# State space steps of an encoder layer: the impulse response moves into the beat of the transposes and outputs

## The chip, the core and the metric

The kernel runs on one core of a Trainium2 chip. The metric is the device time of one execution in microseconds, from start to end of the program on that core; lower is better. The core has a matrix engine (TensorE, PE in the profile, with its weight loads shown apart as PEld), a vector engine (VectorE, DVE), an activation engine (ScalarE, ACT), a general engine (GpSimd, POOL) and an engine that here only issues transfers (SyncE, SP). Each runs its own queue of instructions in order; semaphores tie the queues together.

## The reference

One layer of an encoder is applied to 256 prompt tokens and 512 sample tokens, width 1024. One projection of the normalised input feeds three mixers: a state space model in both directions, differential attention, and attention into 256 memory tokens. Their outputs are weighted by gates and joined, and a feed-forward part follows. The change touches the state space model and runs beside the projection for the gates:

```python
def layer(x, mem, li, ...):
    h = rmsnorm(x, norm_mix_g[li])
    proj = h @ w_in[li]
    u, q, k, v, qm, gl = jnp.split(proj, SPLITS, axis=-1)
    ug = uf.reshape(Bsz, L, S5_GROUPS, S5_GROUP)      # 64 groups of 16 channels
    y_f = s5_direction(ug, ...)                       # forward in time
    y_b = jnp.flip(s5_direction(jnp.flip(ug, axis=1), ...), axis=1)
    y = (y_f + y_b).reshape(Bsz, L, S5_WIDTH) + s5_d[li].astype(F32) * uf
    ...

def s5_direction(u, lam_re, lam_im, log_dt, b_re, b_im, c_re, c_im):
    ...
    bu = jnp.einsum('bcgh,gph->bcgp', u_chunk.astype(jnp.complex64), b_bar)
    a_cum, s = lax.associative_scan(_lin_op, (a, bu), axis=1)   # 64 complex states per group
    y = jnp.einsum('bcgp,ghp->bcgh', s, c).real
```

## The kernel before

Tokens are cut into blocks of eight (96 blocks). Within a block the model is a small matrix, the impulse response; from block to block the states are carried by a scan. The 64 groups are done four at a time, in 16 steps numbered 0 to 15. In class `S5` each step has these parts:

- `fetch` loads the parameters (`par`, three buffers) by SP.
- `build` and `build_e` make the outer products `G` and `E` on VectorE, about six operations of 0.6 to 1.2 us each.
- `response` multiplies `G` with the input matrices on TensorE, 16 matmuls on tiles of 64 rows by 32 columns into two PSUM tiles `psK` (one for each direction). ScalarE copies both into `K`, VectorE adds the diagonal with two short operations, SP stores `K` to memory and reads it back eight times, shifted, as the block matrix `TT`.
- `weights` transposes `E` on TensorE into two PSUM tiles `psE`; ScalarE copies them into `ET`.
- `tables` makes the factors of the scan on ScalarE: `w` and `wr` (four instructions each), `R` (four), `cs` and `sn` (three). `R` has one buffer, so that the next step's `R` is written only when the scan of the step at hand has read it.
- `states` multiplies the inputs by `ET` (8 matmuls into `psI`, one pair of PSUM banks). VectorE rotates the result (`X`, `T`), scans it (`W`, two operations) and rotates it back.
- `outputs` multiplies by `TT` and `G` (12 matmuls into `psY`); ScalarE copies `psY` to `Ysb`, and SP stores it.

`steps` is a generator that strings these together for neighbouring steps and yields three times a round: it calls such a stretch a beat. The first beat of round `s` holds `response(s+1)` and `build_e(s+1)`, the second `states(s)` and `build(s+2)`, the third `outputs(s-1)`, `weights(s+1)` and `tables(s+1)`.

Beside the steps runs the projection for the gates: 72 groups of 24 matmuls (`gl`, 8 slices of the width times three products of high and low halves, 256 tokens wide). A group fills one PSUM bank of a pool of two, ScalarE copies it to `glt` with the bias added, SP stores it. After each group `pace.tick` lets the generator advance by 0.69 beats on average. The weights for `gl` come through `wr`, which ScalarE turns into a high and a low half (`wh`, `wl`, 128x1024 each), two pairs for six groups.

The written order is not the order in which the engines work. A scheduler takes the program as written and orders each engine's queue by when it holds an instruction to be ready; the queues below show what came of it. `keep_in_program_order` ties an instruction behind the one written just before it on its engine. The PSUM tiles `psK`, `psE` and `psY` come from one pool of four banks (`psum(1, b=4, w=1, d=2)`: four banks `b`, one pair `w` for `psI`, two `d` for `u` and `gl`).

Of the kernel before, what the change touches and what calls it, by code (L numbers as in the profile page):

```python
# [20 lines left out]
NK = 99  # L21
# [3 lines left out]
class S5:  # L25
# [313 lines left out]
    def build_e(self, qd):  # L339

        st = self.st[qd]
        st["E"] = self._outer("E", qd, 1, st["B"], st["F"], False)

    def response(self, qd):

        nc, pq, env = self.nc, self.pq, self.env
        st = self.st[qd]
        G = st["G"]

        psK = [env.psb(f"psK{qd}{d}") for d in range(2)]  # L350
        for w in range(2):
            for d in range(2):
                p = slice(64 * d, 64 * d + 64)
                for g in range(4):
                    c = 32 * g + 16 * w
                    nc.tensor.matmul(psK[d][32 * g : 32 * g + 32, 0:128], st["b"][p, c : c + 32],
                                     G[p, w, g].rearrange("p i h -> p (i h)"), start=(w == 0), stop=(w == 1))
        K = pq.tile([128, 240], F32, name=f"K{qd}", tag="K", bufs=1)
        nc.scalar.activation(K[:, 112:240], psK[0][:, 0:128], AF.Copy)
        nc.scalar.activation(K[:, 0:112], psK[1][:, 0:112], AF.Copy)  # L360
        k0 = K[:, 112:128]
        nc.vector.tensor_tensor(out=k0, in0=k0, in1=psK[1][:, 112:128], op=ALU.add)
        nc.vector.tensor_tensor(out=k0, in0=k0, in1=st["diag"], op=ALU.add)
        nc.sync.dma_start(self.k_scr[qd], K)
        kv = self.k_scr[qd].rearrange("(g r) c -> r g c", r=32)[0:16]

        TT = pq.tile([128, 4, 128], F32, name=f"TT{qd}", tag="TT", bufs=3)
        for j in range(8):
            nc.sync.dma_start(TT[16 * j : 16 * j + 16], kv[:, :, 16 * j : 16 * j + 128])
        st["TT"] = TT  # L370

    def weights(self, qd):

        nc, pq, env = self.nc, self.pq, self.env
        st = self.st[qd]
        E = st["E"]
        ET = pq.tile([128, 2, 4, 128], F32, name=f"ET{qd}", tag="ET", bufs=2)
        for c in range(2):
            ps = env.psb(f"psE{qd}{c}")
            for g in range(4):  # L380
                nc.tensor.transpose(ps[:, 128 * g : 128 * g + 128], E[:, c, g], env.ident)
            nc.scalar.activation(ET[:, c].rearrange("p g l -> p (g l)"), ps, AF.Copy)
        st["ET"] = ET

# [30 lines left out]
    def states(self, qd):  # L415
        nc, pq, env = self.nc, self.pq, self.env
        st = self.st[qd]
        mul, add, sub = ALU.mult, ALU.add, ALU.subtract
        vt = lambda o, a, b, op: nc.vector.tensor_tensor(out=o, in0=a, in1=b, op=op)
        mt, q = divmod(qd, 2)  # L420
        if q == 0:
            U = pq.tile([128, 8, NK], F32, name=f"U{mt}", tag="U", bufs=2)
            nc.sync.dma_start(U.rearrange("p g k -> p (g k)"), self.u_scr[mt])
            self.U = U
        U, ET = self.U, st["ET"]
        st["U"] = U
        sn, cs, R = st["tab"]
        ps = env.ps2(f"psI{qd}")
        for c in range(2):
            for g in range(4):  # L430
                nc.tensor.matmul(ps[:, c, NK * g : NK * g + NK], ET[:, c, g], U[:, 4 * q + g],
                                 start=True, stop=True)
        n = 4 * NK
        B3 = [128, 2, n]
        new = lambda tag, bufs: pq.tile(B3, F32, name=f"{tag}{qd}", tag=tag, bufs=bufs)

        X, T = new("X", 3), new("T", 1)
        vt(X, ps[:, :, 0:n], cs.unsqueeze(1).to_broadcast(B3), mul)
        vt(T, ps[:, ::-1, 0:n], sn, mul)
        vt(X, X, T, add)  # L440

        W = new("W", 1)
        Xf, Wf = (x.rearrange("p c k -> p (c k)") for x in (X, W))
        m, f, b = 2 * n, slice(0, 64), slice(64, 128)
        nc.vector.tensor_tensor_scan(out=Wf[f, 1:m], data0=R[f, 0 : m - 1], data1=Xf[f, 0 : m - 1],
                                     initial=0.0, op0=mul, op1=add)
        nc.vector.tensor_tensor_scan(out=Wf[b, m - 2 :: -1], data0=R[b, m - 1 : 0 : -1],
                                     data1=Xf[b, m - 1 : 0 : -1], initial=0.0, op0=mul, op1=add)

        S, T = new("X", 3), new("T", 1)  # L450
        i = slice(1, n - 1)
        vt(S[:, :, i], W[:, :, i], cs[:, i].unsqueeze(1).to_broadcast([128, 2, n - 2]), mul)
        vt(T[:, :, i], W[:, ::-1, i], sn[:, ::-1, i], mul)
        vt(S[:, :, i], S[:, :, i], T[:, :, i], add)
        S = [S[:, c].rearrange("p (g k) -> p g k", g=4)[:, :, 1:98] for c in range(2)]
        st["S"] = S

    def outputs(self, qd, y_scr):
        nc, pq, env = self.nc, self.pq, self.env
        st = self.st.pop(qd)  # L460
        mt, q = divmod(qd, 2)
        i = slice(1, 98)
        U, TT, S = st["U"], st["TT"], st["S"]
        G = st["G"]
        psY = env.psb(f"psY{qd}")
        for g in range(4):
            o = psY[:, 97 * g : 97 * g + 97]
            nc.tensor.matmul(o, TT[:, g], U[:, 4 * q + g, i], start=True, stop=False)
            nc.tensor.matmul(o, G[:, 0, g], S[0][:, g], start=False, stop=False)
            nc.tensor.matmul(o, G[:, 1, g], S[1][:, g], start=False, stop=True)  # L470
        Ysb = pq.tile([128, 4 * 97], F32, name=f"Ysb{qd}", tag="Ysb", bufs=2)
        nc.scalar.activation(Ysb, psY[:, 0 : 4 * 97], AF.Copy)

        nc.sync.dma_start(y_scr[mt][:, 388 * q : 388 * q + 388], Ysb)
# [5 lines left out]
    def steps(self, y_scr):  # L480

        self.st = {}
        n = 16

        def do(f, qd, *a):
            if 0 <= qd < n:
                f(qd, *a)

        for s in range(-3, n + 1):
            do(self.fetch, s + 3)  # L490
            if s < -2:
                continue
            do(self.response, s + 1)
            do(self.build_e, s + 1)
            yield
            do(self.states, s)
            do(self.build, s + 2)
            yield
            do(self.outputs, s - 1, y_scr)
            do(self.weights, s + 1)  # L500
            do(self.tables, s + 1)
            yield

# [1718 lines left out]
```

## Time and profile before

| | us |
|---|---|
| median of 3 runs | 1717.4 (1714.82 to 1717.45) |
| profiled execution | 1715.9 |
| its span, first to last instruction | 1714.1 |
| the stretch in which the state space steps run | about 255 to 590 |
| TensorE busy in 285 to 400, 400 to 500, 500 to 590 | 113.85, 99.45, 89.85 |
| VectorE busy in the same | 104.92, 92.60, 59.55 |
| ScalarE busy in the same | 84.44, 63.47, 45.64 |

A row of the timeline has the start, the length (both in us), the engine, the line, the operation, what is written from what, and how many were merged; brackets hold the idle time before it and who ended that. A row of the waits has who waited for whom, the sum, how many times, and the longest. In the trace a matmul of 32-bit type (`psI`, `psY`, `psK`) appears as two entries, so 8 of them read x16. The granted clock of TensorE is 1.00 throughout. A matmul's length in the trace is modelled; the distance between starts says how fast they follow each other.

### The profile page before, as it was taken

To read this page: it belongs to the slowest core of one execution; us is meant where nothing else is said; L and a number is where in the kernel's file an instruction comes from. 1 tells how busy PE (TensorE), PEld (TensorE's weight loads), DVE (VectorE), ACT (ScalarE), POOL (GpSimd) and SP (SyncE) were. 2 spreads that over 40 slices of the span, in tenths; PEclk is the share of its full clock that TensorE was granted. 3 is DMA by queue.
4 is the path that set the end of the run, shared out by engine and by line. 5 is a ranking of instruction groups with operands and counts; after the bars stand their busy time and mean duration, and the time that the engine had idled before them with its cause. 6 is when DMAs were issued, how large, how long until landed. Compare 5 with 4: busy or idle time off the path is not lost.

```text
span 1714.1 us, 31468 instructions
## 1 busy us (share of the span) xinstructions
PE 1700.2 (99%) x12082; PEld 1624.3 (95%) x12082; DVE 1313.2 (77%) x2383; ACT 931.8 (54%) x1957; POOL 337.1 (20%) x403
## 2 busy tenths in 40 slices
PE   9999999999999999999999999999999999999999
PEld 9999988999999999999989999998889898989897
DVE  6876556999997459889876687792698868687876
ACT  6554536766665357778766564552444545454541
POOL 0040510000000111001210111430114334343420
PEclk9999999999999999999999999999999999999999
DMA  8433456676656446565964445672314448484733
GB/s 298 166 97 102 136 170 151 153 187 176 170 152 165 129 108 144 132 154 135 209 134 131 162 148 171 153 214 72 87 49 115 137 113 192 114 192 115 173 119 108
DMA packets 206758, 250.02 MB, mean 146 GB/s; under 512 B 34272, under 2 KB 162800, under 8 KB 206608
## 3 DMA queue, kind: packets, MB, share of 16 engines
q1 hardware_dynamic: 162896, 155.70, 30.0%
q0 software_dynamic: 32480, 67.01, 20.5%
q10 hardware_dynamic: 11232, 25.31, 4.3%
q8 instruction: 95, 1.56, 0.4%
q14 instruction: 55, 0.45, 0.1%
HBM read 173.51 MB, written 52.17 MB: 132 GB/s over the span
## 4 chain that ended last, share of the span: by engine, by line
PE 81%; issue 10%; DMA 4%; DVE 3%; ACT 1%; POOL 0%; SPq 0%; POOLq 0%; ACTq 0%; DVEq 0%
PE br L846 4%; PE br L847 4%; PE br L848 4%; PE up L846 3%; PE up L847 3%; PE up L848 3%; PE gate L847 3%; PE gate L848 3%; PE gate L846 3%; PE dn L846 3%; PE dn L848 3%; PE dn L847 3%; PE qk L847 3%; PE qk L846 3%; PE qk L848 3%
## 5 line engine op out<-in xcount | busy, mean ns | idle before, releaser
L846 PE MATMUL gl<-Hhi,wh 128*128 128x256 f32 x576 | 164.7, 286 | 0.5 <-ACT glt L1264 0.3
L847 PE MATMUL gl<-Hlo,wh 128*128 128x256 f32 x576 | 160.4, 278 | 0.0
L848 PE MATMUL gl<-Hhi,wl 128*128 128x256 f32 x576 | 160.2, 278 | 0.0
L679 ACT ACTIVATE wh<-wr 128x1024 fp32r<-128x1024 f32 x116 | 122.3, 1056 | 51.7 <-PE u L847 10.8
L683 POOL DMA_DIRECT2D wl<-wr x46 | 40.2, 874 | 463.5 <-ACT wl L682 440.3
L685 DVE TENSOR_TENSOR wl<-wr,wh 128x1024 fp32r<-128x1024 f32 x70 | 85.8, 1227 | 38.7 <-ACT wh L679 37.1
L846 PEld LDWEIGHTS gl<-Hhi,wh 128*128 128x128 f32 x576 | 108.4, 188 | 3.4 <-issue 1.8
L848 PEld LDWEIGHTS gl<-Hhi,wl 128*128 128x128 f32 x576 | 108.8, 189 | 0.0
L847 PEld LDWEIGHTS gl<-Hlo,wh 128*128 128x128 f32 x576 | 108.4, 188 | 0.2 <-issue 0.2
L846 PE MATMUL qk<-wh,Hhi 128*128 128x256 f32 x384 | 107.6, 280 | 0.0
L847 PE MATMUL qk<-wl,Hhi 128*128 128x256 f32 x384 | 107.5, 280 | 0.0
L848 PE MATMUL qk<-wh,Hlo 128*128 128x256 f32 x384 | 107.2, 279 | 0.0
L602 ACT ACTIVATE wh_S<-ws 128x512 fp32r<-128x512 f32 x91 | 53.9, 625 | 67.0 <-PE up L847 27.8
L607 DVE TENSOR_TENSOR wl_S<-ws,wh_S 128x512 fp32r<-128x512 f32 x91 | 67.0, 757 | 28.9 <-ACT wh_S L602 28.8
L846 PEld LDWEIGHTS qk<-wh,Hhi 128*128 128x128 f32 x384 | 72.3, 188 | 0.8
L848 PEld LDWEIGHTS qk<-wh,Hlo 128*128 128x128 f32 x384 | 72.3, 188 | 0.5
L847 PEld LDWEIGHTS qk<-wl,Hhi 128*128 128x128 f32 x384 | 72.2, 188 | 0.5
L1436 ACT ACTIVATE p<-sc,nm 128x512 f32<-128x512 f32 (+1 forms) x96 | 59.0, 617 | 13.2 <-DVE nm L1434 12.8
L1434 DVE TENSOR_REDUCE nm<-sc 128x1 f32<-128x512 f32 (+1 forms) x96 | 56.7, 599 | 11.5 <-PE sc L1428 10.5
L628 POOL TENSOR_TENSOR ws<-wr,ws 128x512 f32<-128x512 f32 x26 | 38.8, 1492 | 126.1 <-DVE wl_S L607 106.8
L602 ACT ACTIVATE wh_A<-wr 128x512 fp32r<-128x512 f32 x65 | 38.1, 623 | 39.0 <-PE up L847 17.3
L1264 ACT ACTIVATE glt<-gl,bg 128x256 f32<-128x256 f32 x72 | 33.6, 466 | 46.4 <-PE gl L848 34.8
(704 smaller groups left out, 6324.9 us busy)
## 6 DMA issues: line engine op xcount, KB each, us to landing
wl<-wr POOLq DMA_DIRECT2D x46, 512.0 KB, 5.6
wr<-in_w_gate_up_dram SPq DMA_DIRECT2D x44, 512.0 KB, 4.1
wr<-in_w_in_dram SPq DMA_DIRECT2D x40, 512.0 KB, 4.8
wr<-in_w_branch_dram SPq DMA_DIRECT2D x24, 512.0 KB, 3.9
wr<-in_w_down_dram SPq DMA_DIRECT2D x22, 512.0 KB, 4.4
gl_scr<-glt SPq DMA_DIRECT2D x72, 128.0 KB, 3.6
wr<-in_w_in_dram SPq DMA_DIRECT2D x32, 256.0 KB, 4.4
wr<-in_w_mem_kv_dram SPq DMA_DIRECT2D x14, 512.0 KB, 5.1
```

The lines of the kernel that those rows point to most:

```text
L602: self.nc.scalar.activation(f(hi), src, AF.Copy)
L607: self.nc.vector.tensor_tensor(out=f(lo), in0=src, in1=f(hi).bitcast(F32), op=ALU.subtract)
L628: gt(out=s4, in0=A12, in1=s2, op=sub)
L679: self.nc.scalar.activation(hi, r, AF.Copy)
L683: self.nc.gpsimd.dma_start(lo, r.bitcast(F32R), accum_op=ALU.add)
L685: self.sub.tensor_tensor(out=lo, in0=r, in1=hi.bitcast(F32), op=ALU.subtract)
L846: pe.matmul(ps, wh, xh, start=start, stop=False)
L847: pe.matmul(ps, wh, xl, start=False, stop=False)
L848: pe.matmul(ps, wl, xh, start=False, stop=stop)
L1264: act.activation(gt[:, 0:n], ps[:, 0:n], AF.Identity, bias=bg[:, M : M + 1])
L1434: v.tensor_reduce(out=nm[:, m : m + 1], in_=ps, axis=AX.X, op=ALU.max, negate=True)
L1436: act.activation(pm[:, 0:n], ps, AF.Exp, bias=nm[:, m : m + 1], accum_out=s1s[:, tt : tt + 1] if m == 0 else s2)
```

## The change

`response(s+1)` leaves the first beat and is written last among TensorE's parts in the third, which now reads `weights(s+1)`, `outputs(s-1)`, `response(s+1)`, `tables(s+1)`. The matmuls of the state space steps are tied to the one written before them on TensorE, by a new helper `pe`; only in the first rounds, while the first third beat is set up, is the first of them left free. Later `gl` matmuls are not tied and can be ordered between.

```diff
+    def pe(self, i):
+
+        if self.joined:
+            self.tc.keep_in_program_order(i)
+        self.joined = True
+
     def response(self, qd):
...
-                    nc.tensor.matmul(psK[d][32 * g : 32 * g + 32, 0:128], st["b"][p, c : c + 32],
-                                     G[p, w, g].rearrange("p i h -> p (i h)"), start=(w == 0), stop=(w == 1))
+                    self.pe(nc.tensor.matmul(psK[d][32 * g : 32 * g + 32, 0:128], st["b"][p, c : c + 32],
+                                             G[p, w, g].rearrange("p i h -> p (i h)"), start=(w == 0), stop=(w == 1)))
...
-                nc.tensor.transpose(ps[:, 128 * g : 128 * g + 128], E[:, c, g], env.ident)
+                self.pe(nc.tensor.transpose(ps[:, 128 * g : 128 * g + 128], E[:, c, g], env.ident))
...
-                nc.tensor.matmul(ps[:, c, NK * g : NK * g + NK], ET[:, c, g], U[:, 4 * q + g],
-                                 start=True, stop=True)
+                self.pe(nc.tensor.matmul(ps[:, c, NK * g : NK * g + NK], ET[:, c, g], U[:, 4 * q + g],
+                                         start=True, stop=True))
...
-            nc.tensor.matmul(o, TT[:, g], U[:, 4 * q + g, i], start=True, stop=False)
-            nc.tensor.matmul(o, G[:, 0, g], S[0][:, g], start=False, stop=False)
-            nc.tensor.matmul(o, G[:, 1, g], S[1][:, g], start=False, stop=True)
+            self.pe(nc.tensor.matmul(o, TT[:, g], U[:, 4 * q + g, i], start=True, stop=False))
+            self.pe(nc.tensor.matmul(o, G[:, 0, g], S[0][:, g], start=False, stop=False))
+            self.pe(nc.tensor.matmul(o, G[:, 1, g], S[1][:, g], start=False, stop=True))
...
             if s < -2:
                 continue
-            do(self.response, s + 1)
             do(self.build_e, s + 1)
             yield
             do(self.states, s)
             do(self.build, s + 2)
             yield
+            self.joined = s > -1
+            do(self.weights, s + 1)
             do(self.outputs, s - 1, y_scr)
-            do(self.weights, s + 1)
+            do(self.response, s + 1)
             do(self.tables, s + 1)
             yield
```

What the queues make of it shows best in step 9. In the rows below, a name's first number is the step (`psK90` and `psK91` are the two response tiles of step 9); the last number only counts tiles. TensorE before, around the response of step 9:

```order
L847 MATMUL gl_489_5949<-Hlo_106,wh21_1_5427 128x256
L848 MATMUL gl_489_5949<-Hhi_105,wl21_1_5428 128x256
L356 MATMUL psK90_490_5979<-G9_5862,par9_5490 32x128 x7
L356 MATMUL psK91_491_5980<-G9_5862,par9_5490 32x128 x4
L356 MATMUL psK90_490_5979<-G9_5862,par9_5490 32x128
L356 MATMUL psK91_491_5980<-G9_5862,par9_5490 32x128 x4
L846 MATMUL gl_493_6020<-Hhi_105,wh21_0_5420 128x256
L847 MATMUL gl_493_6020<-Hlo_106,wh21_0_5420 128x256
```

TensorE after, the end of the outputs of step 7 and the response of step 9:

```order
L474 MATMUL psY7_498_6128<-U3_5528,TT7_5668 128x97
L475 MATMUL psY7_498_6128<-X7_5824,G7_5301 128x97
L476 MATMUL psY7_498_6128<-X7_5824,G7_5301 128x97
L362 MATMUL psK90_499_6144<-G9_5829,par9_5490 32x128 x4
L362 MATMUL psK91_500_6145<-G9_5829,par9_5490 32x128 x4
L362 MATMUL psK90_499_6144<-G9_5829,par9_5490 32x128 x4
L362 MATMUL psK91_500_6145<-G9_5829,par9_5490 32x128 x4
L853 MATMUL gl_502_6200<-Hhi_105,wh22_0_5737 128x256
```

The response stood alone between `gl` groups; now it follows the transposes of step 9 and the outputs of step 7, and three `gl` groups without a break follow it. On ScalarE before, from the table `R` of step 9 to the copies of the second `gl` group behind the transposes:

```order
L404 ACTIVATE R9_6180<-s5kmask_3589,s5rho_111 128x2x99 x4
L472 ACTIVATE Ysb7_6161<-psY7_498_6148 128x388
L382 ACTIVATE ET9_6164<-psE90_499_6165 128x512
L411 ACTIVATE cs10_6442<-wr10_6441,half_pi_87 128x396
L382 ACTIVATE ET9_6164<-psE91_500_6171 128x512
L409 ACTIVATE sn10_6444<-w10_6440 128x396 x2
L403 ACTIVATE wr11_6692<-s5kpos_3588,s5magic_3590,s5v8_110 128x99 x4
L1264 ACTIVATE glt_501_6199<-gl_502_6200,bg_112 128x256
L402 ACTIVATE w11_6691<-s5kpos_3588,s5v8_110 128x99 x4
L1264 ACTIVATE glt_503_6227<-gl_504_6228,bg_112 128x256
```

The same place on ScalarE after:

```order
L388 ACTIVATE ET9_6115<-psE90_496_6116 128x512
L388 ACTIVATE ET9_6115<-psE91_497_6122 128x512
L410 ACTIVATE R9_6180<-s5kmask_3589,s5rho_111 128x2x99 x4
L478 ACTIVATE Ysb7_6141<-psY7_498_6128 128x388
L365 ACTIVATE K9_6162<-psK90_499_6144 128x128
L417 ACTIVATE cs10_6442<-wr10_6441,half_pi_87 128x396
L366 ACTIVATE K9_6162<-psK91_500_6145 128x112
L409 ACTIVATE wr11_6692<-s5kpos_3588,s5magic_3590,s5v8_110 128x99 x2
L415 ACTIVATE sn10_6444<-w10_6440 128x396 x2
L409 ACTIVATE wr11_6692<-s5kpos_3588,s5magic_3590,s5v8_110 128x99 x2
L408 ACTIVATE w11_6691<-s5kpos_3588,s5v8_110 128x99 x4
L1271 ACTIVATE glt_501_6199<-gl_502_6200,bg_112 128x256
```

`ET` moved ahead of `R`, the two copies `K` and the four `w` moved between `R` and the first `glt`. In the steps where the beat comes two `gl` groups after `psI` (`R4`, `R5`, `R7`, `R10`, `R13`) `ET` stays behind `R`. In those of `R3`, `R7` and `R14` two `wh` and a `wl` stand between `R` and the first `glt` after the response as well, in that of `R9` none. TensorE after, in step 4, one of seven whose response is cut by `gl` matmuls (before, `psK40` and `psK41` stood together):

```order
L476 MATMUL psY2_431_4863<-X2_4533,G2_4040 128x97
L362 MATMUL psK40_432_4879<-G4_4538,par4_4199 32x128 x4
L853 MATMUL gl_435_4935<-Hhi_105,wh18_0_4294 128x256
L854 MATMUL gl_435_4935<-Hlo_106,wh18_0_4294 128x256
L855 MATMUL gl_435_4935<-Hhi_105,wl18_0_4295 128x256
L362 MATMUL psK41_433_4880<-G4_4538,par4_4199 32x128 x4
L362 MATMUL psK40_432_4879<-G4_4538,par4_4199 32x128 x4
L362 MATMUL psK41_433_4880<-G4_4538,par4_4199 32x128 x4
```

Three `gl` matmuls moved between the two tiles of the response; in steps 2, 4, 5, 6, 7, 10 and 13 it is 18, 3, 3, 15, 3, 29 and 6 of them. TensorE's order is the old one again from the end of this stretch on. On SP the stores of `K`, `glt` and `Ysb` and the loads of `TT`, `par` and `wr` change places among each other in it; GpSimd's queue is the same.

## The prediction

> **What bounds the kernel now.** I read the page first: the span, the share of each engine and the shares of the chain that ended last.
>
> ```profile
> span 1714.1 us, 31468 instructions
> PE 1700.2 (99%) x12082; PEld 1624.3 (95%) x12082; DVE 1313.2 (77%) x2383; ACT 931.8 (54%) x1957; POOL 337.1 (20%) x403
> PE 81%; issue 10%; DMA 4%; DVE 3%; ACT 1%; POOL 0%; SPq 0%; POOLq 0%; ACTq 0%; DVEq 0%
> ```
>
> TensorE has work for the whole span, so a change counts only where it lengthens or shortens TensorE's own queue: its matmuls, their spacing, and its stops. The order of the program changes only from 255 to 590 us, where the state space steps run inside the gate projection (`gl`). So I asked next who waits for whom in that stretch.
>
> ```profile
> ACT R L404 <- DVE W L447: 37.7, 13, 4.2
> DVE X L419 <- PE psI L431: 19.1, 9, 8.3
> PEld psK L356 <- ACT Ysb L472: 2.1, 3, 1.2
> PE psK L356 <- ACT Ysb L472: 1.4, 2, 1.0
> PEld gl L846 <- ACT glt L1264: 1.2, 3, 0.4
> PE gl L846 <- ACT glt L1264: 0.3, 2, 0.2
> 400.00:500.00 100.00, 99.45 (x986) 97.13 (x986) 92.60 (x111) 63.47 (x148) 6.90 (x8) 1.00 0.65 163
> ```
>
> The first two rows are the loop to keep in mind. VectorE waits for `psI`, ScalarE's table `R` waits for VectorE's scan `W`, 13 times, and everything behind `R` in ScalarE's queue waits with it. The next four are what this costs TensorE today: `psK` lacks a free PSUM bank until `Ysb` is copied out, and `gl` lacks one until `glt` is. The load rows alone give 2.1 + 1.2 = 3.3 us, all four 5.0, with some time counted twice; I take 4.2. The last row (TensorE, weight load, VectorE, ScalarE, GpSimd) has VectorE at 93%: nearly full, but not the bound.
>
> Then one step on TensorE, row by row, and the same step on ScalarE.
>
> ```profile
> 434.89 1.92 PE L431 MATMUL psI<-U,ET 128*128 128x99 f32 x16
> ...
> 439.44 0.35 PE L468 MATMUL psY<-U,TT 128*128 128x97 f32 x2
> ...
> 442.09 1.04 PE L381 MATMUL psE<-ident,E 128*128 128x128 f32 x8
> 442.88 0.36 PE L846 MATMUL gl<-Hhi,wh 128*128 128x256 f32 x1
> 443.08 0.28 PE L847 MATMUL gl<-Hlo,wh 128*128 128x256 f32 x1
> ...
> 448.50 0.28 PE L848 MATMUL gl<-Hhi,wl 128*128 128x256 f32 x1
> 448.71 0.67 PE L356 MATMUL psK<-G,par 64*32 64x128 f32 x32
> 449.50 0.39 PE L846 MATMUL gl<-Hhi,wh 128*128 128x256 f32 x1
> 449.73 0.28 PE L847 MATMUL gl<-Hlo,wh 128*128 128x256 f32 x1
> ...
> 452.23 0.28 PE L848 MATMUL gl<-Hhi,wl 128*128 128x256 f32 x1
> ```
>
> ```profile
> 443.43 1.52 ACT L404 ACTIVATE R<-s5kmask,s5rho 128x198 f32<-128x198 f32 x4 [3.26 <-DVE W L447]
> 444.85 0.47 ACT L472 ACTIVATE Ysb<-psY 128x388 f32<-128x388 f32 x1
> 445.22 0.58 ACT L382 ACTIVATE ET<-psE 128x512 f32<-128x512 f32 x1
> 445.70 0.61 ACT L411 ACTIVATE cs<-wr,half_pi 128x396 f32<-128x396 f32 x1
> 446.22 0.58 ACT L382 ACTIVATE ET<-psE 128x512 f32<-128x512 f32 x1
> 446.70 0.95 ACT L409 ACTIVATE sn<-w 128x396 f32<-128x396 f32 x2
> 447.55 1.54 ACT L403 ACTIVATE wr<-s5kpos,s5magic,s5v 128x99 f32<-128x99 f32 x4
> 448.99 0.46 ACT L1264 ACTIVATE glt<-gl,bg 128x256 f32<-128x256 f32 x1
> 449.35 1.18 ACT L402 ACTIVATE w<-s5kpos,s5v 128x99 f32<-128x99 f32 x4
> 450.42 0.47 ACT L1264 ACTIVATE glt<-gl,bg 128x256 f32<-128x256 f32 x1
> 450.78 0.27 ACT L359 ACTIVATE K<-psK 128x128 f32<-128x128 f32 x1
> 450.94 0.26 ACT L360 ACTIVATE K<-psK 128x112 f32<-128x112 f32 x1
> ```
>
> `R` starts 443.43 - 434.89 = 8.54 us after `psI` began: that is when `W` is done. The `glt` behind it ends at 448.99 + 0.46 = 449.45, and at 449.50 the third `gl` group since the transposes starts. It has two PSUM banks to share with its neighbours, and the gap before it is 0.2 us more than after other `psK` groups. So this walk along ScalarE's queue predicts a TensorE stop to within 0.1 us, and I use it on the new order.
>
> **The change, part by part.** No instruction is added or removed: 16 response, transpose, output and state steps stay, with their copies and DMAs. Four things move.
>
> *One: the old waits of `psK` (gain 4.2 us).* Now the largest looks like this:
>
> ```profile
> 354.52 0.63 PE L356 MATMUL psK<-G,par 64*32 64x128 f32 x14
> 356.12 0.64 PE L356 MATMUL psK<-G,par 64*32 64x128 f32 x18 [0.96 <-ACT Ysb L472]
> ```
>
> In the new order the fifth tile of the four-bank pool waits for the transposes' copy `ET` instead of `Ysb`. Where one `gl` group stands between `psI` and the beat, `ET` now stands ahead of `R` on ScalarE and is done about psI + 6, long before `psK` at psI + 8. Where two groups stand there, `ET` comes behind `R`, at psI + 8.5 + 1.4 + 0.4 + 0.5 = 10.8, and `psK`'s second tile comes at about 11, mostly with a few `gl` matmuls put in ahead. So this wait goes, and the `gl` stops are counted anew below.
>
> *Two: what is late next is `glt` (cost 9.3 us).* After the joined beat three `gl` groups often follow without a break, and the third needs the first one's bank. In the step of `R9`, the new order on ScalarE from `R` to the first `glt` is R, Ysb, K, cs, K, wr, sn, wr, w, glt. From the starts above that is 1.42 + 0.37 + 0.16 + 0.52 + 0.16 + 0.85 + 1.44 + 1.07 + 0.46 = 6.45 us (`ET` left, but `K` and `w` came in). The bank is free at psI + 8.54 + 6.45 = 15.0. TensorE wants it at: `psI` and one `gl` group 4.55 (434.89 to 439.44), outputs and transposes 3.44 (439.44 to 442.88), the response 0.7 (below), two `gl` groups 2.85 + 2.72, together 14.3. Stop: 0.7 us. `R8`, `R11` and `R12` have the same queue, so 4 x 0.7 = 2.8. Where the weight split is in the queue ahead of `glt`, three of its pieces are added:
>
> ```profile
> 336.67 1.05 ACT L679 ACTIVATE wh<-wr 128x1024 fp32r<-128x1024 f32 x1
> 337.62 1.05 ACT L682 ACTIVATE wl<-wr 128x1024 fp32r<-128x1024 f32 x1
> ```
>
> At 0.95 us each they make 2.85. `R3`: 15.0 + 2.85 = 17.85 against 14.3, a stop of 3.5. `R14` has them but neither `wr` nor `w` (-2.5): 1.1. `R7` has them, one `glt` (0.36) and both `ET` (0.96) in front, 19.2, but also one more `gl` group (2.72) and a split response (0.5): 17.5, a stop of 1.7. `R6`: 15.0 against 14.3 + 0.5, 0.2. `R5`, `R10` and `R13` are free by 16.3 to 16.8 against 17.5. Sum: 2.8 + 3.5 + 1.1 + 1.7 + 0.2 = 9.3. All of it rests on `W` at psI + 8.5.
>
> *Three: the response's array shape (cost 2.2 us).* `psK` runs on 64x32 tiles, everything else on 128x128:
>
> ```profile
> 410.13 0.28 PE L848 MATMUL gl<-Hhi,wl 128*128 128x256 f32 x1
> 410.35 0.69 PE L356 MATMUL psK<-G,par 64*32 64x128 f32 x32
> 410.96 0.39 PE L846 MATMUL gl<-Hhi,wh 128*128 128x256 f32 x1
> 411.19 0.28 PE L847 MATMUL gl<-Hlo,wh 128*128 128x256 f32 x1
> ```
>
> Entering takes 0.22 against a spacing of 0.12 (+0.1), leaving +0.2 and then 0.23 against 0.11. Before, the order has 18 `psK` pieces (numbers 0 and 11 in two); after, 24, since numbers 2, 4, 5, 6, 7, 10 and 13 are cut by 3 to 29 `gl` matmuls. Each more costs about 0.1 + 0.3 + 0.1 of its own = 0.5, so 6 x 0.5 = 3.0. Entering from `psY` instead of from `gl`, 16 times, has no row: between the same 0.1 (gain 0) and no cost (gain 1.6). I take the middle, 3.0 - 0.8 = 2.2. The Trainium skill, "TensorEngine Tiling (Array Packing)", Key Properties, says that changing the tiling mode drains TensorE, whatever stands before; by that rule the middle value falls away and this term is 3.0, by issue at pace it is 1.4. The rule speaks against this change.
>
> *Four: the spacing of `gl` (gain 1.2 us).* After transposes it is (448.50 - 443.08) / 46 = 0.118 us, after the response (452.23 - 449.73) / 22 = 0.1135. Before, some 600 `gl` matmuls stand at the slow spacing (18 groups or pairs between a transpose beat and the next `psK`); 600 x 0.0043 = 2.6 us. Now every joined beat ends in `psK`. All fast is a gain of 2.6; if cut responses leave the slow spacing behind them (about 620 `gl` follow those) nothing is gained. Middle: 1.2.
>
> What costs nothing: the response's two copies and two small additions move with it; the additions stand on VectorE behind the transposed step's scan, and in the 13 waits above ScalarE, not VectorE, was late. SP's store of `K` and the reads of `TT` come some 14 us later (response 10 stands at 448.71 now; its transposes, with which it will go, follow those at 442.09 by one step, about 20 us), but `outputs` uses them two steps on, some 36 us; the loads of `par` that stand behind them on SP are needed a step later. GpSimd's queue is unmoved. The start (transposes of step 0 some 9 us earlier) takes two waits off VectorE that no one on TensorE waited for.
>
> Sum: -4.2 + 9.3 + 2.2 - 1.2 = +6.1 us. The profiled execution took 1715.9 us (span 1714.1 and 1.8 around it), so 1722.0. The median of the three runs shown is 1.5 above it, 1717.4: **1723 us**, slower by 0.35%.
>
> **Rivals.** A change of 0.2% (3.4 us) is about what a measurement of this kernel can tell from none.
>
> *Faster: the new `glt` stops don't come.* They decide when `W` is done 0.7 us sooner or the `gl` groups start later; VectorE now gets `psI` one `gl` group later in most steps, with 7% of room. But 8.54 is already `psI` and five VectorE operations in a row with no wait, so I see no way to shorten it. Without them: -4.2 + 2.2 - 2.6 = -4.6, 1713 us.
>
> *No difference to be told:* the stops come at half size (`R3` and `R7`, which rest on the weight split standing ahead of `glt`, shrink), -4.2 + 4.7 + 1.4 - 1.2 = +0.7, 1718 us.
>
> *Much slower: `W` is late.* The wait of `R` had one of 4.2 us, and with `W` at psI + 10 instead of 8.5 each of the eight stopping steps loses 1.5 more and the five with two `gl` groups begin to wait for `ET`: 6.1 + 8 x 1.5 = +18, 1735 us. VectorE at 93% speaks for it, its 9 waits for `psI` against.
>
> **Chances.** Forecast 0.60; faster 0.15; no difference 0.18; much slower 0.07. The range leaves out half of the faster case and the far slower one: 1713 to 1730; the forecast's own range, stops of 6 to 13 us and terms three and four at their ends, is 1719 to 1729. Slower by over 0.2% is the forecast without its lower edge and the late case: 0.62; within 0.2%: 0.22; faster: 0.16.
>
> **What would show it.** In the new profile `psK` waits for `Ysb` are gone; `gl` waits for `glt` grow from about 1.5 to about 9 us, the longest near 3.5 in the step of `R3` (about 337 us); some `psK` rows stand split by `gl` rows; `gl` after the joined beat is spaced 0.113. I am wrong if `gl` hardly waits for `glt`, if `psK` waits for `ET`, or if `R` starts later than psI + 9 in most steps.

## The result, and the profile after

The changed kernel takes **1730.45 us** (median of 5 runs, 1727.65 to 1732.91) against 1716.71 us for the kernel before (5 runs on the same chip, 1714.82 to 1717.45). The ratio is 1.0083, with a 95% interval of 1.0072 to 1.0094: slower by 0.8%, where 0.35% was forecast. The direction and the kind of wait came as forecast. The size was over twice the forecast, and the time lies just above the upper end of the range, 1730.

The profiled execution of the changed kernel took 1727.65 us, the fastest of its five, so its span shows less than the median's loss. The page's span and shares, then four rows of the waits from 255 to 620 us (columns: total us, how often, longest), then the stretch from 400 to 500 us:

```profile
span 1725.9 us, 31460 instructions
PE 1706.1 (99%) x12082; PEld 1628.9 (94%) x12082; DVE 1310.5 (76%) x2383; ACT 933.3 (54%) x1957; POOL 336.8 (20%) x403
...
ACT R L410 <- DVE W L453: 24.5, 11, 3.3
PEld gl L853 <- ACT glt L1271: 12.3, 10, 3.6
PE gl L853 <- ACT glt L1271: 10.3, 9, 3.4
...
400.00:500.00 100.00, 96.88 (x956) 93.96 (x955) 87.53 (x111) 61.76 (x143) 6.02 (x7) 1.00 0.58 153
```

The rows of `psK` waiting for `Ysb` are gone, as forecast. The rows of `gl` waiting for `glt` have grown from 1.2 us to 12.3. TensorE executes 956 matmuls in the 100 us where it executed 986 before, and is busy for 96.9 of them instead of 99.5; VectorE falls from 93 to 88 and ScalarE from 63 to 62. No engine is fuller than it was: TensorE stands still more often, and for a short while, shown further down, it runs at half its clock. The span grew by 11.8 us. From the first matmul into `u` to the first into `qk`, the attention's, it is 380.2 us before (204.7 to 584.9) and 394.4 after (203.3 to 597.7): 14.3 more, near the 13.7 by which the medians differ. The rest of the span, where the order is the same, is 2.5 us shorter in this execution. So the loss is all in that stretch, and it is larger there than the spans show.

The step of `R9`, which the prediction walked through, on ScalarE:

```profile
451.10 1.52 ACT L410 ACTIVATE R<-s5kmask,s5rho 128x198 f32<-128x198 f32 x4 [2.20 <-DVE W L453]
452.52 0.47 ACT L478 ACTIVATE Ysb<-psY 128x388 f32<-128x388 f32 x1
...
453.31 0.63 ACT L417 ACTIVATE cs<-wr,half_pi 128x396 f32<-128x396 f32 x1 [0.15 <-DVE X L425]
...
454.71 0.94 ACT L415 ACTIVATE sn<-w 128x396 f32<-128x396 f32 x2
...
456.28 1.17 ACT L408 ACTIVATE w<-s5kpos,s5v 128x99 f32<-128x99 f32 x4
457.35 0.81 ACT L1271 ACTIVATE glt<-gl,bg 128x256 f32<-128x256 f32 x2
```

And on TensorE, the stop of the step before, the state products, and the stop of this step:

```profile
438.78 0.28 PE L854 MATMUL gl<-Hlo,wh 128*128 128x256 f32 x1
438.90 0.28 PE L855 MATMUL gl<-Hhi,wl 128*128 128x256 f32 x1
439.73 0.39 PE L853 MATMUL gl<-Hhi,wh 128*128 128x256 f32 x1 [0.55 <-ACT glt L1271]
...
442.00 0.28 PE L854 MATMUL gl<-Hlo,wh 128*128 128x256 f32 x1
442.11 0.28 PE L855 MATMUL gl<-Hhi,wl 128*128 128x256 f32 x1
...
442.57 1.92 PE L437 MATMUL psI<-U,ET 128*128 128x99 f32 x16
...
445.06 0.28 PE L853 MATMUL gl<-Hhi,wh 128*128 128x256 f32 x1
445.18 0.28 PE L854 MATMUL gl<-Hlo,wh 128*128 128x256 f32 x1
...
457.04 0.28 PE L855 MATMUL gl<-Hhi,wl 128*128 128x256 f32 x1
457.86 0.39 PE L853 MATMUL gl<-Hhi,wh 128*128 128x256 f32 x1 [0.54 <-ACT glt L1271]
```

`R` starts 451.10 - 442.57 = 8.53 us after `psI` (8.54 was used). The first of the two `glt` is done about 457.8, that is psI + 15.2 (15.0 was computed), and the third `gl` group since the beat, ready at 457.16, starts at 457.86: a stop of 0.70 us, where 0.7 was forecast. (TensorE, too, is later than computed: 457.16 is psI + 14.6, and 14.3 was computed. The two differences nearly cancel, so that a match this close is partly luck.)

### The profile page after: what moved, and what is told of

Same layout as the page of the kernel before. It is cut to its first block, busy times and chain, and to the rows that moved or that the text cites. A ratio compares the mean times of both kernels' runs of the same rounds, so it can differ in the third digit from the quotient of the medians.

```text
span 1725.9 us, 31460 instructions
## 1 busy us (share of the span) xinstructions
PE 1706.1 (99%) x12082; PEld 1628.9 (94%) x12082; DVE 1310.5 (76%) x2383; ACT 933.3 (54%) x1957; POOL 336.8 (20%) x403
## 5 line engine op out<-in xcount | busy, mean ns | idle before, releaser
L853 PEld LDWEIGHTS gl<-Hhi,wh 128*128 128x128 f32 x576 | 108.9, 189 | 16.8 <-ACT glt L1271 12.3
L1443 ACT ACTIVATE p<-sc,nm 128x512 f32<-128x512 f32 (+1 forms) x96 | 59.0, 617 | 13.8 <-DVE nm L1441 13.2
```

What stands on the lines that cost most here:

```text
L853: pe.matmul(ps, wh, xh, start=start, stop=False)
L1443: act.activation(pm[:, 0:n], ps, AF.Exp, bias=nm[:, m : m + 1], accum_out=s1s[:, tt : tt + 1] if m == 0 else s2)
```

## Experiments

Three parts are mixed in the change: the response *joins* the beat, the state steps' matmuls are *tied* to the written order, and the *tables* on ScalarE, which nobody touched, meet both. The runs take them apart. Times are medians; the ratio to the kernel before, run beside it on the same chip, has its 95% interval. The kernel before stood at 1715.8 to 1716.7 us in all of them.

### The wait of R taken away: it passes on

In the changed kernel `R` leaves the tables and is written at the start of its own step, held there in ScalarE's order, so that by then `W` of the step before is done.

```diff
+    def decay(self, qd):
+        R = self.pq.tile([128, 2, 4, NK], F32, name=f"R{qd}", tag="R", bufs=1)
+        for g in range(4):
+            c = slice(4 * qd + g, 4 * qd + g + 1)
+            self.tc.keep_in_program_order(self.nc.scalar.activation(R[:, :, g], ...))
...
-            pin(nc.scalar.activation(R[:, :, g], ...))
...
             if s < -2:
                 continue
+            do(self.decay, s)
             do(self.build_e, s + 1)
```

> The changed kernel, with the table R alone taken out of the tables and written at the start of the next round, tied behind the gl copies that stand before it on ScalarE. If the cost is gl waiting for its copy glt, which stands on ScalarE behind R and so behind VectorE's scan W (theory one), TensorE's waits for glt fall from about 12 us to under 3 and the time falls by about 11 us, to about 1719. If the cost is the cut responses and the drains of the array (theory two), only the pieces count (24 to 20): about 2 us less, 1728.

Measured: 1728.24 us, ratio 1.0067 [1.0050, 1.0084]. Theory one's number is missed: nearly nothing came back. Theory two's, 1728, is met, and the trace has its 20 pieces; from the matmul ahead of each to the one behind it they take 15.0 us in all, against 17.1 in the 24 of the changed kernel. So what came back fits the pieces, and the stops are untouched. The waits of this run, and two rows of ScalarE in the same step:

```profile
ACT cs L413 <- DVE X L431: 18.3, 12, 2.2
PEld gl L860 <- ACT glt L1278: 12.2, 9, 3.9
...
451.31 0.63 ACT L413 ACTIVATE cs<-wr,half_pi 128x396 f32<-128x396 f32 x1 [1.59 <-DVE X L431]
...
455.36 0.82 ACT L1278 ACTIVATE glt<-gl,bg 128x256 f32<-128x256 f32 x2
```

`R` no longer waits, but the cosine table `cs`, next in line, now does: it has two buffers, and the one it needs is read by VectorE's last rotation `X` of the same chain. `glt` stands behind it as before, and the stops stay at 12.2 us. The wait for `W` was only the first of two on one chain.

The same edit on the kernel before:

> The same move of R on the kernel before. Theory one: the 4.2 us in which psK waited for Ysb and gl for glt mostly go, 3 us less, about 1713.5. Theory two: 18 pieces as before, no change, 1716.7.

Measured: 1715.85 us, ratio 0.9996 [0.9987, 1.0005]: no change that can be told, as theory two had it. So `R` alone is not what the old waits hang on either.

### The order without its ties

The changed kernel with the new order as written, but with `pe` handing the matmul through, so that none is held in place:

```diff
     def pe(self, i):
-        if self.joined:
-            self.tc.keep_in_program_order(i)
-        self.joined = True
+        return i
```

> The changed kernel without its ties: the response is written in the joined beat, but nothing is kept in program order. R still stands ahead of the gl copies on ScalarE. Theory one: nearly all of the loss stays, 1725 to 1730. Rival (the ties are what costs): back to the kernel before, 1717.

Measured: 1717.54 us, ratio 1.0007 [0.9998, 1.0017]. The rival is right and theory one's number a miss: the change costs almost nothing on balance as long as nothing is tied. The waits row, then TensorE and ScalarE in the same step:

```profile
PEld gl L851 <- ACT glt L1269: 1.0, 1, 1.0
...
448.72 0.28 PE L853 MATMUL gl<-Hhi,wl 128*128 128x256 f32 x1
448.83 1.47 PE L435 MATMUL psI<-U,ET 128*128 128x99 f32 x12
450.09 0.36 PE L851 MATMUL gl<-Hhi,wh 128*128 128x256 f32 x1
...
449.31 0.81 ACT L1269 ACTIVATE glt<-gl,bg 128x256 f32<-128x256 f32 x2
```

ScalarE's queue from `R` to `glt` is the same as with ties, and no shorter. But here 12 of the 16 matmuls that the trace shows for `psI` stand between the second and the third `gl` group. They take 1.26 us (448.83 to 450.09), the first `glt` is done about 449.8, and the third group finds its bank free. Tied, `psI` stands behind the third group, and three groups follow without a break: that is the order in which the stop arises.

### The ties without the joining

The reverse: the kernel before, its response in a beat of its own, with the same ties.

```diff
+            self.joined = s > -1
             do(self.outputs, s - 1, y_scr)
             do(self.weights, s + 1)
             do(self.tables, s + 1)
```

(beside `pe` and its calls, as in the change).

> The kernel before with the ties alone: the response keeps its own beat, and the matmuls of the steps are kept in program order. 22 pieces of responses in place of 18 cost about 2 us; ScalarE's queue is nearly the one before. Theory one: 1717 to 1720. Rival (the ties are what costs): 1725 or more.

Measured: 1723.62 us, ratio 1.0042 [1.0027, 1.0057]: half of the loss without any joining, with stops of the same kind. It lies between theory one's range (up to 1720) and the rival's (from 1725), so neither is met: the ties alone cost a part, not all.

```profile
PEld gl L854 <- ACT glt L1272: 9.6, 11, 3.3
```

### Which ties

The changed kernel with every tie but those of `psI` (its call of `pe` becomes the plain matmul), and then with those of `psI` alone.

> The changed kernel with the ties on the response, the transposes and the outputs, but none on the state products psI, which then stand up to one gl group earlier in the last rounds (psI12 six matmuls after the second group instead of after the third). Theory one (psI held behind the gl group written before it makes the chain psI, X, W and so the copies glt late): the stops of glt shrink to under 4 us and the time is 1717 to 1720. Theory two (the ties on transposes and outputs cost it): stops of glt stay at about 12 us, 1727 to 1730.

> The changed kernel with ties on the state products psI alone; transposes, outputs and response go where the scheduler puts them. Theory one (the tie on psI costs it): 1725 to 1730, with stops of glt of about 8 to 12 us. Theory two (the other ties do): about 1718, as without any tie (1717.5).

Measured: 1721.06 us, ratio 1.0033 [1.0021, 1.0044], without the ties of `psI`; 1726.43 us, 1.0058 [1.0045, 1.0071], with them alone. The rows of the waits, of the first run and then of the second:

```profile
PEld psK L362 <- ACT ET L388: 4.6, 3, 2.6
PEld gl L853 <- ACT glt L1271: 1.1, 3, 0.7
```

```profile
PEld gl L857 <- ACT glt L1275: 7.8, 4, 2.4
```

So the ties of `psI` carry most of the loss, and without them the stops of `glt` shrink to 1.1 us, as theory one has it. The first run is 1 us above its expectation, since another wait came: three times the transposes' copy `ET` comes late on ScalarE, and `psK`, tied, needs the bank that `ET` empties. Behind the longest of these stops the granted clock is 0.50 for 3.4 us (358.4 to 361.8), which the last section comes back to. (The prediction named this wait as a sign that it was wrong; in the changed kernel itself it doesn't appear.)

### The tables moved out of the way

All of the tables' work on ScalarE is written behind the state products and held in that order, with a second buffer for `R`; the ties and the joined beat stay (the last two operations, on `wr` and `cs`, are held like `sn`).

```diff
-        R = pq.tile([128, 2, 4, NK], F32, name=f"R{qd}", tag="R", bufs=1)
+        R = pq.tile([128, 2, 4, NK], F32, name=f"R{qd}", tag="R", bufs=2)
...
-        pin = self.tc.keep_in_program_order if qd == 0 else lambda i: i
+        pin = self.tc.keep_in_program_order
...
-            nc.scalar.activation(sn[:, c], f2(w), AF.Sin, scale=sg)
+            pin(nc.scalar.activation(sn[:, c], f2(w), AF.Sin, scale=sg))
...
             do(self.build, s + 2)
+            do(self.tables, s + 1)
...
-            do(self.tables, s + 1)
```

> The changed kernel with all of the tables' ScalarE work (w, wr, R, sn, cs) written behind the state products and held in that order, and R in two buffers, so that neither R nor cs stands ahead of the copies glt waiting for VectorE; the ties and the joined beat stay. Theory one (the loss is ScalarE's wait for the chain from psI, in R or in cs, with glt queued behind it): the stops of glt fall from 12.5 us to under 3 and the time is 1717 to 1720. If the wait passes on to a third instruction, as it passed from R to cs: 1726 to 1730. A rival (the loss is in the response's 24 pieces and the spacing of the gl matmuls, not in the stops): 1725 or more, with the stops gone.

> The same edit of the tables on the kernel before. Theory one: its 4 us of waits of psK and gl (Ysb and glt behind R) go: 1712 to 1714. If they are set by something else, as R alone moved late suggested (1715.9): 1715 to 1717. With the tables behind the fourth group's copy late themselves: over 1718.

Measured: 1716.58 us, ratio 1.0005 [0.9996, 1.0014], on the changed kernel, and 1711.99 us, 0.9976 [0.9967, 0.9985], on the kernel before. The second is at the lower edge of what theory one expects; the first is 0.4 us below its bounds. What is left of the waits, the changed kernel first:

```profile
PEld psK L362 <- ACT ET L388: 0.8, 1, 0.8
```

```profile
PEld gl L846 <- ACT glt L1264: 1.0, 5, 0.2
```

On the changed kernel no row of `gl` waiting for `glt` is left at all. The changed kernel stood 13.7 us above the kernel before and now stands 0.8 above it: 12.9 us were the price of how ScalarE's tables stand. On the kernel before the same tables cost 3.8 us. (The new place, the fixed order and the second buffer for `R` came in one edit; what each is worth alone was not tried.)

### With the tables moved: ties or joining?

4.6 us still lie between the two. The other two kernels with the tables moved: the joined beat without ties, and the ties without the joined beat.

> The changed kernel with the tables moved as in the run before on it (held in order behind the state products, R in two buffers) and without the ties. With the tables moved, the changed kernel stood at 1716.6 and the kernel before at 1712.0. Theory one (the ties cost nothing once nothing in ScalarE's queue waits for VectorE; the 4.6 us left are the joined beat's: more pieces of the response and its other neighbours): 1715 to 1717.5. Rival (the ties themselves cost the rest): 1711.5 to 1713.5.

> The kernel before, the response in its beat of its own, with the ties and with the tables moved. With the ties alone it stood at 1723.6, with the moved tables alone at 1712.0. Theory one: the ties cost nothing without the stops: 1711 to 1713.5. Rival (the ties themselves cost the 4.6 us between the two kernels with moved tables): 1715 to 1717.

Measured: 1717.94 us, ratio 1.0015 [1.0006, 1.0024], 0.4 above theory one's bounds, and 1711.80 us, 0.9977 [0.9969, 0.9986], within them. The whole picture:

| us | as before | ties alone | joined alone | joined and tied |
|---|---|---|---|---|
| tables as they were | 1716.7 | 1723.6 | 1717.5 | 1730.5 |
| tables moved | 1712.0 | 1711.8 | 1717.9 | 1716.6 |

In the upper row, each against the kernel before that ran beside it, the ties cost 7.4 us, joining 1.3, and both 13.7: far more than their sum. In the lower row, reckoned in the same way, the ties cost nothing, and joining costs 5.2 us with them and 5.5 without. (Joined without ties, the kernel gains nothing by moved tables, since it had one stop of 1.0 us left to lose. That joining costs less in the upper row fits this: there it also takes away the old waits, which the moved tables take away in the lower one.) So the lower row has the response alone to explain. In the traces of the joined kernel without ties and of the tied one without joining (spans 1715.6 and 1710.1) the time from the matmul ahead of a `psK` piece to the one behind it, summed over all pieces, is 20.0 us in 24 pieces against 14.1 in 18; the difference, 5.9, is about that of the spans, 5.5.

### The response first

If it is the cuts, the response should be written where it is not cut. In the joined beat its second tile is the fifth for four banks and has to wait. Written first, it is the outputs that wait for the bank, and `gl` matmuls put in among them run on the same 128x128 array as they do.

```diff
             self.joined = s > -1
+            do(self.response, s + 1)
             do(self.weights, s + 1)
             do(self.outputs, s - 1, y_scr)
-            do(self.response, s + 1)
```

> The changed kernel with the tables moved and the response written first in the joined beat, ahead of transposes and outputs, the ties kept. The response is then whole in every step (18 pieces, all cuts at the start), and outputs that wait for a bank are cut at no price, being of the gl matmuls' own shape. Theory one (the 4.6 to 6.1 us that joining costs once the stops are gone are the cut responses): 1711 to 1713.5, as the kernel before with moved tables (1712.0). Rival (the price is in joining itself, wherever the response stands): 1715.5 to 1718.

> The changed kernel with the response written first in the joined beat and nothing else, the ties kept. The outputs now float behind the first or second gl group and stand between the groups; from R to the first copy glt ScalarE has R, cs, wr, sn, Ysb, glt, 5.1 us against the 6.45 of the prediction, so the bank is free at psI + 13.6 against 14.3. Theory one (the loss is the stops of glt and the cut responses): 1714 to 1719. Rival (the beat joined under ties costs whatever its order): 1725 or more.

Measured with the tables moved: **1711.33 us, ratio 0.9971 [0.9960, 0.9982]**, the fastest of all kernels here, though not told apart from the two at 1712. The response has 18 pieces and its sum is 13.8 us; joining costs nothing once the response is whole. Without moving the tables: 1725.02 us, ratio 1.0049 [1.0036, 1.0061], a miss of 6 us. The waits, then ScalarE in the step of `R9`:

```profile
PEld gl L853 <- ACT glt L1271: 9.2, 8, 2.7
ACT cs L417 <- DVE X L425: 3.7, 5, 0.8
...
450.13 1.51 ACT L410 ACTIVATE R<-s5kmask,s5rho 128x198 f32<-128x198 f32 x4 [1.45 <-DVE W L453]
452.42 0.63 ACT L417 ACTIVATE cs<-wr,half_pi 128x396 f32<-128x396 f32 x1 [0.78 <-DVE X L425]
...
455.77 0.46 ACT L1271 ACTIVATE glt<-gl,bg 128x256 f32<-128x256 f32 x1
```

From `R` to the end of `glt` it is 6.1 us, not 5.1: the wait of `cs`, seen in the first run, was left out of the expectation again, and 0.78 us of it count in full. The whole response does its part (its sum is 13.8 us, 3.3 less than in the changed kernel), but the stops need the tables moved. And two of these stops are followed by 3.4 us each at a granted clock of 0.50 (from 314.3 and from 420.1), in which TensorE loses about 3 us; no expectation had that.

## Why the prediction was right and wrong

**Right: where the time goes.** The time was forecast to move from `psK`'s wait for `Ysb` to `gl`'s wait for `glt` behind `R`, with `W` at psI + 8.5, and it did. The longest stop was to be 3.5 us in the step of `R3`; it is the second of these rows, 3.5 us later than the matmul before it allows:

```profile
320.40 0.38 PE L853 MATMUL gl<-Hhi,wh 128*128 128x256 f32 x1 [1.35 <-ACT glt L1271]
341.38 0.58 PE L853 MATMUL gl<-Hhi,wh 128*128 128x256 f32 x1 [3.38 <-ACT glt L1271]
```

**Term one, the old waits (-4.2): right, and 3.8 by the starts.** Their rows are gone. From the matmul ahead of a `psK` piece to the one behind it, the 18 pieces take 17.9 us in the kernel before, waits included, and 14.1 in the tied kernel with its own beat and moved tables, which has next to none.

**Term two, the stops of `glt` (+9.3): this is the step that failed.** It was right in kind and 4 us too small: 11.8 us of stops came by the starts of the matmuls (12.3 by the load row), and 1.5 us more behind the longest of them. `R3` (3.5), `R8`, `R9` and `R12` (0.7 each) are as forecast; `R7` came at 1.5 for 1.7, `R14` at 1.5 for 1.1, `R6` at 0.7 for 0.2 and `R11` at 0.9 for 0.7.

The first thing that failed is the list of steps: the prediction gave none to `R2`, and that is the first row above, a stop of 1.5 us. There `W` isn't late at all:

```profile
313.90 1.52 ACT L410 ACTIVATE R<-s5kmask,s5rho 128x198 f32<-128x198 f32 x4
315.31 0.63 ACT L417 ACTIVATE cs<-wr,half_pi 128x396 f32<-128x396 f32 x1
...
319.86 0.85 ACT L1271 ACTIVATE glt<-gl,bg 128x256 f32<-128x256 f32 x2
```

`R` starts without a wait, behind a queue that is already full of tables, weight copies and `ET`. The prediction looked for ScalarE being late through VectorE, and not for ScalarE being late by itself.

The second is what a stop does to the matmuls behind it, which the prediction put at nothing. Here are the stretch behind the stop of `R3` (the value after the count of GpSimd is the granted clock), the same stretch of time in the kernel before, and two of the matmuls:

```profile
341.20:344.60 3.40, 3.22 (x15) 3.22 (x16) 1.07 (x2) 1.86 (x4) 0.86 (x1) 0.50 1.08 222
...
341.20:344.60 3.40, 3.40 (x30) 3.26 (x30) 3.37 (x6) 2.91 (x9) 0.86 (x1) 1.00 0.88 187
...
342.19 0.41 PE L853 MATMUL gl<-Hhi,wh 128*128 128x256 f32 x1
342.40 0.41 PE L854 MATMUL gl<-Hlo,wh 128*128 128x256 f32 x1
```

The clock is granted at half for 3.4 us, the `gl` matmuls follow each other at 0.213 us instead of 0.113, and TensorE executes 15 where it executed 30. That is about 1.5 us on top of the stop, and no row of the waits shows it.

**Term three, the response's shape (+2.2): too small.** The unknown was what entering from `psY` costs, and the middle was taken between nothing and the price of entering from `gl`. Here it is, in the changed kernel:

```profile
311.53 0.39 PE L475 MATMUL psY<-X,G 128*128 128x97 f32 x2
311.76 0.39 PE L476 MATMUL psY<-X,G 128*128 128x97 f32 x2
312.07 0.42 PE L362 MATMUL psK<-G,par 64*32 64x128 f32 x8
312.43 0.39 PE L853 MATMUL gl<-Hhi,wh 128*128 128x256 f32 x1
```

The second `psY` matmul of the pair starts about 0.11 after the first, at 311.87, and `psK` 0.20 after it; the mean over 14 entries is 0.205 us, against 0.207 from `gl`. (The prediction counted 16 such entries.) So the upper end, 3.0, was the one to take: the sum over the pieces is 17.1 us in the 24 of the changed kernel, none of which waits for a bank, against the 14.1 in 18, 0.5 a piece as priced. The Trainium skill, "TensorEngine Tiling (Array Packing)", Key Properties, has TensorE drain at every change of the tiling mode, and the trace agrees: entering takes 0.20 us from either neighbour, against 0.11 to 0.12 without a change of shape.

**Term four, the spacing of `gl` (-1.2): wrong in sign.** The rule that the response leaves `gl` at 0.113 us doesn't hold. 805 of 1615 `gl` intervals are at the slow spacing now and 642 of 1628 were before: +0.8 us. In the TensorE rows of the result, the `gl` matmuls behind a joined beat stand 0.12 apart up to the stop at 439.73, 0.113 apart behind it, and 0.12 apart again behind `psI`.

The terms as they came, in the stretch from `u` to `qk`: -3.8 + 11.8 + 1.5 + 3.0 + 0.8 = 13.3, of the 14.3 us by which it grew; the last 1.0 was not broken up. Forecast was 6.1. The misses are 4.0 in term two, 2.0 in term four, 0.8 in term three and 0.4 in term one, all on the same side: steps that weren't walked, a clock taken as constant, and twice the middle between two bounds.

**The rival cases.** The faster one and the one without a difference needed the stops of `glt` to stay away or to come at half size; they came larger. The much slower one (`W` late) didn't come: from `R3` on, `R` starts at psI + 8.5 in every step. What the prediction didn't see is which part of the change makes the order that it walked through. It treated the fixed order as given; by the table of the experiments, the ties turn a joining that costs 1.3 us into one that costs 13.7, because they keep `psI` from standing between the second and the third `gl` group.

**Open.** What switches the spacing of `gl` between 0.113 and 0.118 us was not tried. Of the 4.6 us between the changed kernel and the kernel before, both with moved tables, the two profiled executions show 0.6 (1713.1, the fastest of its eleven, and 1712.5), of which the stretch from `u` to `qk` has 2.1 the one way and the rest of the span 1.5 the other.

## What to carry to other kernels

An order that is fixed by hand takes away the work that a scheduler would have put into a gap; walk every step of the new order along the queue of the engine that empties the banks, and count that engine's own load too, not only its waits. A stop of TensorE can cost more than its length: here 3.4 us at half clock followed most stops of over 2.1 us. A wait is rarely alone: removing `R`'s left the stops as they were, behind `cs`, and only moving the whole table behind the copies that TensorE needs brought 3.8 us on the old kernel and 12.9 on the new one. Work in another array shape is to be written where it isn't cut, since each cut costs about 0.5 us in the changed kernel (8 and 24 matmuls), and more where the halves are alike: in the joined kernel without ties and with moved tables, 16 and 16 take 1.55 us, where 8 and 24 take 1.33 in the changed one and a whole response takes 0.80.

## What was not expected of the hardware

The granted clock drops to 0.50 in the middle of a busy stretch. Over the fourteen traces, ten stops between 255 and 600 us are longer than 2.1 us from start to start (2.16 to 4.03). In eight cases 3.4 us at half clock begin near the end of the stop or up to 1.5 us behind it (6.8 at the 3.26 us of the kernel with ties alone); behind two stops of 2.26 us nothing follows, though it does behind those of 2.16 and 2.19, and there is none behind a stop under 2.1. The other eight traces have no such stop in this stretch, and their clock stays at 1.00 there. What decides was not tried.

The spacing of the same matmul (128x256 on the whole array) has two values, 0.113 and 0.118 us, and it changes at stops and at other matmuls in either direction: behind a whole response it is 0.118 in the changed kernel and 0.113 in the one without ties, at the same granted clock of 1.00. The rows of TensorE behind the response of the same step, with the ties and then without:

```profile
452.09 0.28 PE L855 MATMUL gl<-Hhi,wl 128*128 128x256 f32 x1
452.21 0.28 PE L853 MATMUL gl<-Hhi,wh 128*128 128x256 f32 x1
```

```profile
444.75 0.28 PE L851 MATMUL gl<-Hhi,wh 128*128 128x256 f32 x1
444.86 0.28 PE L852 MATMUL gl<-Hlo,wh 128*128 128x256 f32 x1
```

With half of its 1600 intervals at the slow value this stretch loses some 4 us to it (800 x 0.0047), as much as the longest stop here, and no row of the waits shows it.
